# Tying late readers behind the newest weight split in a hybrid mLSTM / DeltaNet block

## The chip, the cores and the metric

One Trainium2 core runs the whole kernel as one program. The time is device time in microseconds (us) of one execution, from a few repeated runs; a separate profiled execution gives the trace. The engines are TensorE (PE, with its weight loads shown as PEld), VectorE (DVE), ScalarE (ACT), GpSimd (POOL) and SyncE (SP), which here does nothing but issue DMA transfers. Each engine works through its own queue of instructions in a fixed order: an instruction that waits holds up all behind it on its engine.

## What is computed

A decoder block on x of 512 tokens by 2048 channels, all in float32. One input projection of the normalized x feeds an mLSTM branch (8 heads), a gated DeltaNet branch (16 heads) and two gates; one output projection brings each branch back to 2048 channels.

```python
u = _rmsnorm(h, norm_w)
proj = jnp.matmul(u, w_in)                 # 2048 x 20528
# mLSTM: q, k, v, o, z, i, f       DeltaNet: q, k, v, z, b, a       gates: a, b
...
h_a = _rmsnorm(_mlstm_chunkwise(...)) * ml_norm_w * sigmoid(ml_o) * silu(ml_z)
...
dq, dk, dv = split(_causal_conv_silu(dn_qkv, dn_conv_w), 3)
h_b = _rmsnorm(_gated_delta_chunkwise(l2(dq), l2(dk), dv, beta, g), dn_norm_w) * silu(dn_z)
...
y = sigmoid(gate_a) * (h_a @ w_out[:2048]) + sigmoid(gate_b) * (h_b @ w_out[2048:])
out = _rmsnorm(x + y, final_norm_w)
```

The delta rule solves, for each chunk, a unit lower triangular system; `_causal_conv_silu` is a depthwise convolution over 4 tokens followed by SiLU.

## The kernel before

**Products with split weights.** Each float32 matrix product is made of three products of rounded parts: a tile `raw` is loaded (`load_raw`, L146), ACT writes its rounded copy `hi` (`split_hi`, L113, tile wh), DVE the remainder `lo` (`split_lo`, L116, tile wl). `next_w` (L158) hands out the parts of block i and, before that, traces the loads up to block i+4 and the splits up to block i+3. There are four buffers of each, so split i+3 needs PE to be through block i-1. Splits and loads carry a high priority.

**Order of the work.** UNITS lists four mLSTM units (two heads each) and eight DeltaNet units (two heads each), as mLSTM, DeltaNet, DeltaNet, four times. A DeltaNet unit (`dn_unit`, L698) projects K, Q, V and Z one after the other with `proj_cm` (L201): each is 16 ticks long, and a tick follows each six products (L212 to L214). All other work of the heads is written as Python generators. `start(gen, wait)` puts one on a list; `tick()` resumes those that are due, and what a generator yields is the number of ticks until its next step. So the small work is traced in between the projections' products.

PE's order is the order of this text (`manual_schedule` for PE). The orders of ACT, DVE, POOL and of SP's transfers are made by a planner at build time: it simulates the engines' times and, whenever an engine is free, takes the ready instruction with the highest priority, which is the place in the text, moved forward by `urgent()` and `high_priority`. An instruction may therefore be issued long before its place in the text, if the simulation finds it ready and the engine free. On the chip the order is fixed, and semaphores do the waiting.

**A DeltaNet unit.** `conv_silu` (L436) copies a projection from PSUM (L440, tile yp, on ACT), convolves on DVE (L441, L443), takes tanh on ACT (L446) and finishes SiLU on DVE (L447). `turn` (L464) transposes blocks on DVE and lets `travel` (L471) carry them through DRAM (td) to the other layout. `dn_front_k` (L488), started 4 ticks after K, loads a row to all partitions (gb), masks it on POOL (L493) and takes exponentials on ACT (L495, L499) for the decay tile dm; multiplies K by itself (L510, tile pk); scales (L512, L526, tile aq); sends the 32x32 diagonal blocks through DRAM (ld, L529; ls, L539); solves the triangular systems on DVE in 31 steps of two operations (L549, L551, tiles tmp and xi), two steps per tick; sends the result through DRAM again (xd, L559; tt, L560), and 10 ticks later transposes it (L563, tile tn). `dn_front_q` makes K by Q (L571, L574). `dn_back` (L580), started 4 ticks after Z, takes Q's norms on ACT (L462, tile njk), joins the 32x32 inverses to 128x128 ones by four groups of small products (L604, L615, L616, L626, L633), the results of each going through ACT (L609 and so on, tiles s), scales V (L638), and starts `dn_chain` for each head (L656 to L679: products pr, pw, pst, po). `gated` (L482) multiplies a head's output by its gate and stores it; it is started 12 ticks after the output's `turn`.

**An mLSTM unit.** `ml_prep` (L731) loads two rows, masks, takes exponentials (em, L740) and multiplies K by Q (L745); `ml_rec` (L757) runs the recurrence over four chunks (pnum, pcs, c) and normalizes; `ml_fin` turns the result and starts `gated`.

**At the start**, x is loaded, its sums of squares are taken, each row block is scaled (L281 to L285: DVE, POOL, then DVE and ACT for one half each), and PE transposes it (L291). The first raw tiles are loaded in the same time.

PSUM has three banks for projections (pj), three for small products (wk) and two more (o).

Of the kernel before, what the change touches and what calls it, by code (L numbers as in the profile page):

```python
# [15 lines left out]
P = 128  # L16
S = 512
NC = S // P
# [30 lines left out]
def hybrid_body(  # L49
# [59 lines left out]
        V.tensor_scalar(out=convc, in0=pt[:, 64:256], scalar1=0.5, scalar2=None, op0=ALU.mult)  # L109


    def split_hi(hi, src):
        A.copy(hi, src)  # L113

    def split_lo(lo, src, hi):
        V.tensor_tensor(out=lo, in0=src, in1=hi.bitcast(F32), op=ALU.subtract)  # L116


    plan = []
# [49 lines left out]
    def urgent(level=1):  # L169
        return tc.high_priority(offset=level * PRIO)  # L170
# [4 lines left out]
    def start(gen, wait=0):  # L175
        active.append([gen, clock["t"] + wait])
# [96 lines left out]
    for c in range(NC):  # L273
        xt = xts[c]
        jk = p0.tile([P, HD], F32, tag="jk", name="jk", bufs=2)
        A.activation(jk, xt[:, 0:HD], AF.Square, accum_out=ss[:, c, 0:1])
        jv = p0.tile([P, HD], F32, tag="jv", name="jv", bufs=2)
        V.scalar_tensor_tensor(out=jv, in0=xt[:, HD:D], scalar=1.0, in1=xt[:, HD:D], op0=ALU.mult, op1=ALU.mult,
                               accum_out=ss[:, c, 1:2])
        V.tensor_tensor(out=rs[:, c:c + 1], in0=ss[:, c, 0:1], in1=ss[:, c, 1:2], op=ALU.add)  # L280
        V.tensor_scalar(out=rs[:, c:c + 1], in0=rs[:, c:c + 1], scalar1=1.0 / D, scalar2=EPS,  # L281
                        op0=ALU.mult, op1=ALU.add)
        G.tensor_tensor(out=rs[:, c:c + 1], in0=rs[:, c:c + 1], in1=mhalf[:, c:c + 1], op=ALU.pow)
        V.tensor_scalar(out=xt[:, 0:HD], in0=xt[:, 0:HD], scalar1=rs[:, c:c + 1], scalar2=None, op0=ALU.mult)
        A.mul(xt[:, HD:D], xt[:, HD:D], rs[:, c:c + 1])  # L285

    def make_u(kt):
        pool, tg = ((psw, "wk"), (pso, "o"))[kt % 2]
# [139 lines left out]
    def row_bcast(r, name):  # L428
        t = wk.tile([P, NC, P], F32, tag="rb", name=name, bufs=3)
        nc.sync.dma_start(t.rearrange("p c t -> p (c t)"), rows_d[r, :].partition_broadcast(P))  # L430
        return t

    def bc(col, n):
        return col.unsqueeze(2).to_broadcast([P, NC, n])

    def conv_silu(ps, ct, dst):  # L436
        yp = yps[cnt["yp"] % NYP]
        cnt["yp"] += 1
        with urgent():
            A.copy(yp[:, 3:S + 3], ps)  # L440
        V.tensor_scalar(out=dst, in0=yp[:, 3:S + 3], scalar1=convc[:, 144 + ct:145 + ct], scalar2=None, op0=ALU.mult)  # L441
        for j in (2, 1, 0):
            V.scalar_tensor_tensor(out=dst, in0=yp[:, j:j + S], scalar=convc[:, 48 * j + ct:48 * j + ct + 1], in1=dst,  # L443
                                   op0=ALU.mult, op1=ALU.add)
# [12 lines left out]
    def token_norms(pk, dst):  # L457

        jk = wk.tile([P, P], F32, tag="jk", name="njk", bufs=1)
        for c in range(NC):  # L460
            with urgent():
                A.activation(jk, pk[:, c, :], AF.Square, accum_out=dst[:, c:c + 1])  # L462
# [17 lines left out]
        yield 1  # L480

    def gated(hn, w, g, kt):  # L482
        V.scalar_tensor_tensor(out=g, in0=hn.rearrange("p c t -> p (c t)"), scalar=w, in1=g, op0=ALU.mult,
                               op1=ALU.mult)
        nc.sync.dma_start(h_d[kt], g)
        yield 1

    def dn_front_k(hs, kq, u):  # L488
        for j in range(2):
            h = hs[j]  # L490
            rb = row_bcast(16 + h, "gb")
            dm = wk.tile([P, NC, P], F32, tag="dm", name="dm")
            G.affine_select(out=dm, in_=rb, pattern=[[0, NC], [1, P]], channel_multiplier=-1, base=0,  # L493
                            compare_op=ALU.is_ge, fill=-1e30)
            A.activation(rb, rb, AF.Exp)  # L495
            ge = wk.tile([P, NC], F32, tag="ge", name="ge", bufs=4)
            V.tensor_copy(ge, rb[:, :, P - 1])
            for c in range(NC):
                A.activation(dm[:, c, :], dm[:, c, :], AF.Exp, bias=ngam[:, c, h:h + 1])  # L499
# [41 lines left out]
        G.memset(xi, 0.0)  # L541
        for q in range(4):
            G.memset(xi.rearrange("p m t -> p (m t)")[q * NSYS:(q + 1) * NSYS, q:(BS // 4) * BS:BS + 4], 1.0)
        yield 4
        for i in range(BS - 1):
            n, m = BS - 1 - i, i // 4 + 1
            tmp = wk.tile([P, 80], F32, tag="tmp", name="tmp")
            tv = tmp[:, 0:n * m].rearrange("p (a b) -> p a b", b=n)
            V.tensor_tensor(out=tv, in0=ls[:, i, i + 1:BS].unsqueeze(1).to_broadcast([P, m, n]),  # L549
                            in1=xi[:, 0:m, i].unsqueeze(2).to_broadcast([P, m, n]), op=ALU.mult)  # L550
            V.tensor_tensor(out=xi[:, 0:m, i + 1:BS], in0=xi[:, 0:m, i + 1:BS], in1=tv, op=ALU.subtract)  # L551
            if i % 2:
                yield 1
# [5 lines left out]
                nc.sync.dma_start(xd[:, :, :, q, :].rearrange("g b m t -> (g b) m t"), xi[q * NSYS:(q + 1) * NSYS])  # L559
            nc.sync.dma_start(tt, xd.rearrange("g b m q t -> (b m q) g t"))  # L560
        yield 10
        with urgent():
            V.transpose(tn.rearrange("p g m -> p (g m)"), tt.rearrange("p g t -> p (g t)"))  # L563
        u.update(tn=tn, tt=tt)

# [14 lines left out]
    def dn_back(hs, kq, u):  # L580

        qe = wk.tile([P, 2, NC], F32, tag="qe", name="qe")
        for j in range(2):
            token_norms(u["qn"][j], qe[:, j, :])
        V.tensor_scalar(out=qe, in0=qe, scalar1=EPS, scalar2=EPS * P, op0=ALU.add, op1=ALU.mult)
        u["qe"] = qe
        for j in range(2):
# [47 lines left out]
            V.tensor_copy(tb[0:64, :, 64:128], p4[0:64])  # L635
        for j in range(2):
            vn = u["vs"][j]
            V.tensor_tensor(out=vn, in0=vn, in1=bc(u["nk"][:, j, :], P), op=ALU.mult)  # L638
        start(dn_chain(0, hs, kq, u), 2)
        start(dn_chain(1, hs, kq, u), 3)  # L640

# [56 lines left out]
    def dn_unit(p):  # L698
        hs = (2 * p, 2 * p + 1)
        dcol = p * NB  # L700
        u = {"aq": [], "qt": [], "ke": [], "vs": [], "g": [], "dm": []}
        kq = [wk.tile([P, 2, S], F32, tag="kq", name=f"kq{h}", bufs=4) for h in hs]
        ps = proj_cm(DN_K + dcol)
        for j in range(2):
            conv_silu(ps[j], 16 + hs[j], kq[j][:, 0, :])
            ke = wk.tile([P, NC, P], F32, tag="ke", name="ke", bufs=4)
            turn(kq[j][:, 0, :], ke)
            u["ke"].append(ke)
        start(dn_front_k(hs, kq, u), KWAIT)
        ps = proj_cm(DN_Q + dcol)  # L710
        u["qn"] = []
        for j in range(2):
            conv_silu(ps[j], hs[j], kq[j][:, 1, :])
            qn = wp.tile([P, NC, P], F32, tag="tg", name="qn", bufs=3)
            turn(kq[j][:, 1, :], qn)
            u["qn"].append(qn)
        start(dn_front_q(hs, kq, u), QWAIT)
        ps = proj_cm(DN_V + dcol)
        for j in range(2):
            vt = wk.tile([P, NC, P], F32, tag="vn", name="vt", bufs=4)  # L720
            conv_silu(ps[j], 32 + hs[j], vt.rearrange("p c t -> p (c t)"))
            turn(vt, vt)
            u["vs"].append(vt)
# [33 lines left out]
    def ml_rec(j, hs, kq, u):  # L757
# [2 lines left out]
        kT = kq[j][:, 0, :]  # L760
        w, we, de, qi = u["em"][j]
        kw = u["kw"][j]
        V.tensor_tensor(out=kw, in0=kw, in1=bc(we, P), op=ALU.mult)
        sq = wk.tile([P, NC], F32, tag="sq", name="sq")
        c1 = None
        for c in range(NC):
# [242 lines left out]
```

## Time and profile before

| what | us |
|---|---|
| median of 3 runs | 2394.93 (2393.64 to 2398.55) |
| the profiled execution's own time | 2400.5 |
| its span, first to last instruction | 2398.5 |
| mean granted clock of TensorE | 0.987 |
| DVE busy | 1144.5 |
| ACT busy | 800.1 |

A row of the timeline reads: start in us from the span's start, length, engine (a q behind it is the queue that issues transfers), line of the kernel, operation, tile written <- tiles read, shape, count, and in brackets the idle time of the engine just before and what ended it. A row of the waits reads: who waited <- for whom: us in all, times, the longest. A row of a group of instructions reads: line, engine, operation, tiles, shape and count | busy us, mean ns of one | idle us before and its releasers. A row of a stretch reads: from:to, length, then for PE, PEld, DVE, ACT and POOL the busy us (and instructions), then the granted clock of PE, the DMA share and GB/s.

### The profile page before, as it was taken

The numbers are of one execution on the slowest core, as the hardware profiler recorded it, in microseconds if no ns is written. First come the engines' busy times: TensorE is split into PE (matmuls) and PEld (weight loads), VectorE is DVE, ScalarE is ACT, GpSimd is POOL, SyncE is SP. The second block draws the span as 40 slices with busy tenths as digits, with TensorE's granted clock in tenths as the row PEclk, the third lists the DMA queues.
The fourth block names the chain that finished last, engine by engine and source line by source line (L and its number), as shares of the span: only waits on it lengthen the run. The fifth ranks groups of instructions, "written<-read, shape, count | busy, mean of one in ns | idle before, by whom it ended". The sixth has DMA issues, their size and how long they took to land.

```text
span 2398.5 us, 32163 instructions
## 1 busy us (share of the span) xinstructions
PE 2311.6 (96%) x11647; PEld 1927.6 (80%) x11647; DVE 1144.5 (48%) x2347; ACT 800.1 (33%) x1702; POOL 192.6 (8%) x261
## 2 busy tenths in 40 slices
PE   6999989999998999999899999989999999999998
PEld 5888768788877888887787888778998888888886
DVE  4532857433385744248573425847333222434334
ACT  4323333332333433234242323423333322322222
POOL 0000102100010200002020001011000000010010
PEclk9999989999999999999999999999999999999999
DMA  5533645443364645336563534646375543633433
GB/s 145 129 97 101 152 121 143 125 128 97 101 147 123 159 112 132 97 99 154 128 162 96 141 97 108 149 120 156 99 247 148 158 114 116 213 116 119 128 115 130
DMA packets 465441, 313.12 MB, mean 131 GB/s; under 512 B 234113, under 2 KB 404322, under 8 KB 465282
## 3 DMA queue, kind: packets, MB, share of 16 engines
q1 hardware_dynamic: 465218, 311.01, 48.3%
q8 instruction: 91, 1.49, 0.3%
q14 instruction: 68, 0.56, 0.1%
q10 hardware_dynamic: 64, 0.07, 0.0%
HBM read 264.77 MB, written 46.20 MB: 130 GB/s over the span
## 4 chain that ended last, share of the span: by engine, by line
PE 80%; DMA 6%; DVE 6%; SPq 4%; issue 2%; ACT 1%; POOL 0%; DVEq 0%; POOLq 0%; ACTq 0%
PE pj L212 13%; PE pj L213 12%; PE pj L214 12%; PE py L944 5%; PE py L943 5%; PE py L942 5%; PE pg L242 4%; PE pg L243 4%; PE pg L244 4%; PE pv L243 2%; PE pv L244 2%; PE pv L242 2%; SPq L476 2%; PE pjt L227 1%; PE pjt L229 1%
## 5 line engine op out<-in xcount | busy, mean ns | idle before, releaser
L116 DVE TENSOR_TENSOR wl<-wr,wh 128x512 fp32r<-128x512 f32 x768 | 538.3, 703 | 849.8 <-ACT wh L113 835.5
L113 ACT CAST wh<-wr 128x512 fp32r<-128x512 f32 x768 | 475.8, 621 | 1237.8 <-PE pj L213 588.1
L212 PE MATMUL pj<-uh,wh 128*128 128x512 f32 x1792 | 735.2, 410 | 10.3 <-ACT yp L440 7.0
L214 PE MATMUL pj<-uh,wl 128*128 128x512 f32 x1792 | 706.3, 394 | 0.0
L213 PE MATMUL pj<-ul,wh 128*128 128x512 f32 x1792 | 706.1, 394 | 0.0
L212 PEld LDWEIGHTS pj<-uh,wh 128*128 128x128 f32 x1792 | 341.6, 191 | 81.4 <-ACT yp L440 10.7
L214 PEld LDWEIGHTS pj<-uh,wl 128*128 128x128 f32 x1792 | 340.6, 190 | 74.3
L213 PEld LDWEIGHTS pj<-ul,wh 128*128 128x128 f32 x1792 | 341.4, 191 | 64.1
L942 PE MATMUL py<-wh,hh 128*128 128x512 f32 x512 | 199.2, 389 | 0.0
L943 PE MATMUL py<-wl,hh 128*128 128x512 f32 x512 | 199.2, 389 | 0.0
L944 PE MATMUL py<-wh,hl 128*128 128x512 f32 x512 | 199.2, 389 | 0.0
L242 PE MATMUL pg<-wh,uh 128*128 128x512 f32 x384 | 149.4, 389 | 0.0
L243 PE MATMUL pg<-wl,uh 128*128 128x512 f32 x384 | 149.4, 389 | 0.0
L244 PE MATMUL pg<-wh,ul 128*128 128x512 f32 x384 | 149.4, 389 | 0.0
L943 PEld LDWEIGHTS py<-wl,hh 128*128 128x128 f32 x512 | 96.1, 188 | 20.1
L942 PEld LDWEIGHTS py<-wh,hh 128*128 128x128 f32 x512 | 96.1, 188 | 20.0
L944 PEld LDWEIGHTS py<-wh,hl 128*128 128x128 f32 x512 | 96.1, 188 | 19.8
L242 PE MATMUL pv<-wh,uh 128*128 128x512 f32 x256 | 99.6, 389 | 0.0
L243 PE MATMUL pv<-wl,uh 128*128 128x512 f32 x256 | 99.6, 389 | 0.0
L244 PE MATMUL pv<-wh,ul 128*128 128x512 f32 x256 | 99.6, 389 | 0.0
L244 PEld LDWEIGHTS pg<-wh,ul 128*128 128x128 f32 x384 | 72.1, 188 | 15.1
L242 PEld LDWEIGHTS pg<-wh,uh 128*128 128x128 f32 x384 | 72.1, 188 | 14.9
(243 smaller groups left out, 2328.2 us busy)
## 6 DMA issues: line engine op xcount, KB each, us to landing
wr<-in_w_in_dram SPq DMA_DIRECT2D x640, 256.0 KB, 2.8
wr<-in_w_out_dram SPq DMA_DIRECT2D x128, 256.0 KB, 3.0
td<-to SPq DMA_DIRECT2D x128, 64.0 KB, 2.0
hr<-h_d SPq DMA_DIRECT2D x32, 256.0 KB, 3.5
tgl<-tg_d SPq DMA_DIRECT2D x32, 256.0 KB, 3.1
tg_d<-tgw SPq DMA_DIRECT2D x24, 256.0 KB, 3.3
xt<-in_x_dram SPq DMA_DIRECT2D x8, 512.0 KB, 7.9
gb<-rows_d SPq DMA_DIRECT2D x16, 256.0 KB, 3.9
```

What stands on the lines that cost most here:

```text
L113: A.copy(hi, src)
L116: V.tensor_tensor(out=lo, in0=src, in1=hi.bitcast(F32), op=ALU.subtract)
L212: T.matmul(ps[j], hi[:, k, wsl], uh[:, kt, :], start=(kt == 0), stop=False)
L213: T.matmul(ps[j], hi[:, k, wsl], ul[:, kt, :], start=False, stop=False)
L214: T.matmul(ps[j], lo[:, k, wsl], uh[:, kt, :], start=False, stop=(kt == KT - 1))
L242: T.matmul(ps[c], uh[:, kt, tsl], hi[:, 0, :], start=(kt == 0), stop=False)
L243: T.matmul(ps[c], uh[:, kt, tsl], lo[:, 0, :], start=False, stop=False)
L244: T.matmul(ps[c], ul[:, kt, tsl], hi[:, 0, :], start=False, stop=(kt == KT - 1))
L476: nc.sync.dma_start(d[:, :, a, :].rearrange("m r c -> r m c"), ov[a * BS:(a + 1) * BS])
L942: T.matmul(ps[c], hh[base][:, kt, tsl], hi[:, 0, :], start=(kt == 0), stop=False)
L943: T.matmul(ps[c], hh[base][:, kt, tsl], lo[:, 0, :], start=False, stop=False)
L944: T.matmul(ps[c], hl[base][:, kt, tsl], hi[:, 0, :], start=False, stop=(kt == KT - 1))
```

## The change

`newest` keeps, for ACT and for DVE, the last split traced so far (at the start: the last scaling of x). `behind(engine)` puts what its block traces behind that instruction in the engine's order, at build time; it adds no instruction and no semaphore. The tie applies to the place in the text: at a tick within block i, the newest split is that of block i+3.

```diff
+    newest = {}
+
     def split_hi(hi, src):
-        A.copy(hi, src)
+        newest["A"] = A.copy(hi, src).ins
 
     def split_lo(lo, src, hi):
-        V.tensor_tensor(out=lo, in0=src, in1=hi.bitcast(F32), op=ALU.subtract)
+        newest["V"] = V.tensor_tensor(out=lo, in0=src, in1=hi.bitcast(F32), op=ALU.subtract).ins
+
+    def behind(eng):
+
+        return tc.issue_after(newest[eng])
...
-            split_hi(hi, raw)
-            split_lo(lo, raw, hi)
+            with ExitStack() as first:
+                if not parts:
+                    first.enter_context(behind("V"))
+                    first.enter_context(behind("A"))
+                split_hi(hi, raw)
+                split_lo(lo, raw, hi)
...
+    def silu_end(dst, then=None):
         th = wk.tile([P, S], F32, tag="th", name="th", bufs=3)
-        A.activation(th, dst, AF.Tanh)
+        with behind("A"):
+            A.activation(th, dst, AF.Tanh)
         V.scalar_tensor_tensor(out=dst, in0=th, scalar=1.0, in1=dst, op0=ALU.add, op1=ALU.mult)
+        if then is not None:
+            turn(*then)
+        yield 1
...
     def dn_front_k(hs, kq, u):
-        for j in range(2):
-            h = hs[j]
-            rb = row_bcast(16 + h, "gb")
+        rbs = [row_bcast(16 + h, "gb") for h in hs]
+        yield 4
+        for j in range(2):
             dm = wk.tile([P, NC, P], F32, tag="dm", name="dm")
-            G.affine_select(out=dm, in_=rb, ...)
-            A.activation(rb, rb, AF.Exp)
+            G.affine_select(out=dm, in_=rbs[j], ...)
+            u["dm"].append(dm)
+        yield 2
+        for j in range(2):
+            h, rb, dm = hs[j], rbs[j], u["dm"][j]
             ge = wk.tile([P, NC], F32, tag="ge", name="ge", bufs=4)
-            V.tensor_copy(ge, rb[:, :, P - 1])
-            for c in range(NC):
-                A.activation(dm[:, c, :], dm[:, c, :], AF.Exp, bias=ngam[:, c, h:h + 1])
-            u["dm"].append((dm, rb, ge))
+            with behind("A"):
+                for c in range(NC):
+                    A.activation(dm[:, c, :], dm[:, c, :], AF.Exp, bias=ngam[:, c, h:h + 1])
+                A.activation(rb, rb, AF.Exp)
+            G.tensor_copy(ge, rb[:, :, P - 1])
+            u["dm"][j] = (dm, rb, ge)
...
-        yield 4
+        yield 7
         for i in range(BS - 1):
...
-            V.tensor_tensor(out=tv, in0=ls..., in1=xi..., op=ALU.mult)
+            with behind("V"):
+                V.tensor_tensor(out=tv, in0=ls..., in1=xi..., op=ALU.mult)
...
         yield 10
-        with urgent():
+        with urgent(), behind("V"):
             V.transpose(tn..., tt...)
...
     def dn_unit(p):
...
         for j in range(2):
+            ke = wk.tile([P, NC, P], F32, tag="ke", name="ke", bufs=4)
+            u["ke"].append(ke)
             conv_silu(ps[j], 16 + hs[j], kq[j][:, 0, :])
-            ke = wk.tile([P, NC, P], F32, tag="ke", name="ke", bufs=4)
-            turn(kq[j][:, 0, :], ke)
-            u["ke"].append(ke)
-        start(dn_front_k(hs, kq, u), KWAIT)
+            start(silu_end(kq[j][:, 0, :], (kq[j][:, 0, :], ke)), 3 + 2 * j)
+        start(dn_front_k(hs, kq, u), 1)
...
     def ml_prep(j, hs, kq, u):
...
         iwb = row_bcast(8 + h, "iwb")
+        yield 4
         em = wk.tile([P, NC, P], F32, tag="dm", name="em")
         G.affine_select(out=em, in_=rb, ...)
-        for c in range(NC):
-            A.activation(em[:, c, :], em[:, c, :], AF.Exp, bias=acol[:, c, h:h + 1])
-        yield 4
+        yield 2
+        with behind("A"):
+            for c in range(NC):
+                A.activation(em[:, c, :], em[:, c, :], AF.Exp, bias=acol[:, c, h:h + 1])
+        yield 2
```

Q and V of a DeltaNet unit end in the same way as K: the convolution stays at its place, and `silu_end` with the `turn` follows 3 and 5 ticks later for the two heads. These operations are tied as well, unmoved in the text: `gated`'s multiplication (L483), the scaling of V in `dn_back` (L638) and of K in `ml_rec` (L763), all behind DVE's newest split, and the norms in `dn_back` (L462) behind ACT's. The last scalings of x (L284, L285) are set as `newest` at the start, so that the first weight split is tied behind them.

More of the change, by code (lines that the diff above doesn't have):

```diff
@@ L283, in hybrid_body @@
         G.tensor_tensor(out=rs[:, c:c + 1], in0=rs[:, c:c + 1], in1=mhalf[:, c:c + 1], op=ALU.pow)
-        V.tensor_scalar(out=xt[:, 0:HD], in0=xt[:, 0:HD], scalar1=rs[:, c:c + 1], scalar2=None, op0=ALU.mult)
-        A.mul(xt[:, HD:D], xt[:, HD:D], rs[:, c:c + 1])
+        newest["V"] = V.tensor_scalar(out=xt[:, 0:HD], in0=xt[:, 0:HD], scalar1=rs[:, c:c + 1], scalar2=None,
+                                    op0=ALU.mult).ins
+        newest["A"] = A.mul(xt[:, HD:D], xt[:, HD:D], rs[:, c:c + 1]).ins
     def make_u(kt):
@@ L482, in gated @@
     def gated(hn, w, g, kt):
-        V.scalar_tensor_tensor(out=g, in0=hn.rearrange("p c t -> p (c t)"), scalar=w, in1=g, op0=ALU.mult,
-                               op1=ALU.mult)
+        with behind("V"):
+            V.scalar_tensor_tensor(out=g, in0=hn.rearrange("p c t -> p (c t)"), scalar=w, in1=g, op0=ALU.mult,
+                                   op1=ALU.mult)
         nc.sync.dma_start(h_d[kt], g)
@@ L488, in dn_front_k @@
     def dn_front_k(hs, kq, u):
+        rbs = [row_bcast(16 + h, "gb") for h in hs]
+        yield 4
         for j in range(2):
-            h = hs[j]
-            rb = row_bcast(16 + h, "gb")
             dm = wk.tile([P, NC, P], F32, tag="dm", name="dm")
-            G.affine_select(out=dm, in_=rb, pattern=[[0, NC], [1, P]], channel_multiplier=-1, base=0,
+            G.affine_select(out=dm, in_=rbs[j], pattern=[[0, NC], [1, P]], channel_multiplier=-1, base=0,
                             compare_op=ALU.is_ge, fill=-1e30)
-            A.activation(rb, rb, AF.Exp)
+            u["dm"].append(dm)
+        yield 2
+        for j in range(2):
+            h, rb, dm = hs[j], rbs[j], u["dm"][j]
             ge = wk.tile([P, NC], F32, tag="ge", name="ge", bufs=4)
-            V.tensor_copy(ge, rb[:, :, P - 1])
-            for c in range(NC):
-                A.activation(dm[:, c, :], dm[:, c, :], AF.Exp, bias=ngam[:, c, h:h + 1])
-            u["dm"].append((dm, rb, ge))
+            with behind("A"):
[4 more added lines that the diff above has]
+            u["dm"][j] = (dm, rb, ge)
         nk = wk.tile([P, 2, NC], F32, tag="nk", name="nk")
@@ L548, in dn_front_k @@
             tv = tmp[:, 0:n * m].rearrange("p (a b) -> p a b", b=n)
-            V.tensor_tensor(out=tv, in0=ls[:, i, i + 1:BS].unsqueeze(1).to_broadcast([P, m, n]),
-                            in1=xi[:, 0:m, i].unsqueeze(2).to_broadcast([P, m, n]), op=ALU.mult)
+            with behind("V"):
+                V.tensor_tensor(out=tv, in0=ls[:, i, i + 1:BS].unsqueeze(1).to_broadcast([P, m, n]),
+                                in1=xi[:, 0:m, i].unsqueeze(2).to_broadcast([P, m, n]), op=ALU.mult)
             V.tensor_tensor(out=xi[:, 0:m, i + 1:BS], in0=xi[:, 0:m, i + 1:BS], in1=tv, op=ALU.subtract)
@@ L582, in dn_back @@
         qe = wk.tile([P, 2, NC], F32, tag="qe", name="qe")
-        for j in range(2):
-            token_norms(u["qn"][j], qe[:, j, :])
+        with behind("A"):
+            for j in range(2):
+                token_norms(u["qn"][j], qe[:, j, :])
         V.tensor_scalar(out=qe, in0=qe, scalar1=EPS, scalar2=EPS * P, op0=ALU.add, op1=ALU.mult)
@@ L637, in dn_back @@
             vn = u["vs"][j]
-            V.tensor_tensor(out=vn, in0=vn, in1=bc(u["nk"][:, j, :], P), op=ALU.mult)
+            with behind("V"):
+                V.tensor_tensor(out=vn, in0=vn, in1=bc(u["nk"][:, j, :], P), op=ALU.mult)
         start(dn_chain(0, hs, kq, u), 2)
@@ L714, in dn_unit @@
             qn = wp.tile([P, NC, P], F32, tag="tg", name="qn", bufs=3)
-            turn(kq[j][:, 1, :], qn)
             u["qn"].append(qn)
+            start(silu_end(kq[j][:, 1, :], (kq[j][:, 1, :], qn)), 3 + 2 * j)
         start(dn_front_q(hs, kq, u), QWAIT)
@@ L720, in dn_unit @@
             vt = wk.tile([P, NC, P], F32, tag="vn", name="vt", bufs=4)
+            u["vs"].append(vt)
             conv_silu(ps[j], 32 + hs[j], vt.rearrange("p c t -> p (c t)"))
-            turn(vt, vt)
-            u["vs"].append(vt)
+            start(silu_end(vt.rearrange("p c t -> p (c t)"), (vt, vt)), 3 + 2 * j)
         ps = proj_cm(DN_Z + dcol)
@@ L738, in ml_prep @@
                         compare_op=ALU.is_ge, fill=-1e30)
-        for c in range(NC):
-            A.activation(em[:, c, :], em[:, c, :], AF.Exp, bias=acol[:, c, h:h + 1])
-        yield 4
+        yield 2
+        with behind("A"):
+            for c in range(NC):
+                A.activation(em[:, c, :], em[:, c, :], AF.Exp, bias=acol[:, c, h:h + 1])
+        yield 2
         psc = psw.tile([P, NC, P], F32, tag="wk", name="psc")
@@ L762, in ml_rec @@
         kw = u["kw"][j]
-        V.tensor_tensor(out=kw, in0=kw, in1=bc(we, P), op=ALU.mult)
+        with behind("V"):
+            V.tensor_tensor(out=kw, in0=kw, in1=bc(we, P), op=ALU.mult)
         sq = wk.tile([P, NC], F32, tag="sq", name="sq")
```

## The prediction

> **What bounds the kernel now.** I read the page first, for who is busy, and then the waits of the tensor engine, for where it is not.
>
> ```profile
> span 2398.5 us, 32163 instructions
> ...
> PE 2311.6 (96%) x11647; PEld 1927.6 (80%) x11647; DVE 1144.5 (48%) x2347; ACT 800.1 (33%) x1702; POOL 192.6 (8%) x261
> ```
>
> PE is busy for 2311.6 of 2398.5 us, so only what makes PE wait, or run slowly, can be won. None of the waits below is for a weight split: the splits run three blocks ahead.
>
> ```profile
> PE p L604 <- DVE tn L563: 33.7, 7, 8.1
> ...
> PE pnum L770 <- DVE c L780: 7.8, 4, 3.0
> PE pj L212 <- ACT yp L440: 7.0, 7, 2.5
> PE put L291 <- DVE xt L284: 5.6, 1, 5.6
> PE pj L212 <- ACT thz L454: 3.1, 2, 1.7
> ```
>
> The largest is L604, the first product of dn_back: it waits for tn, the end of the triangular solve, in 7 of 8 DeltaNet units. The timeline of PE shows the worst one (first DeltaNet unit, behind an mLSTM unit):
>
> ```profile
> 327.36 0.39 PE L214 MATMUL pj<-uh,wl 128*128 128x512 f32 x1
> 335.88 1.06 PE L604 MATMUL p<-tn,aq 32*32 32x32 f32 x32 [8.13 <-DVE tn L563]
> ...
> 337.46 0.63 PE L213 MATMUL pj<-ul,wh 128*128 128x512 f32 x1
> 337.89 0.63 PE L214 MATMUL pj<-uh,wl 128*128 128x512 f32 x1
> ...
> 341.26 0.39 PE L213 MATMUL pj<-ul,wh 128*128 128x512 f32 x1
> 341.49 0.40 PE L214 MATMUL pj<-uh,wl 128*128 128x512 f32 x1
> ```
>
> The columns are start and length. Matmuls overlap, so the pace is start to start: 341.49-341.26 = 0.23 us at speed, 337.89-337.46 = 0.43 just after the stall. Some 9 products between 337.46 and 341.26 run at the slow pace, 9 x 0.20 = 1.8 us on top of the 8.1. A tick (six products) is 6 x 0.23 = 1.4 us.
>
> Why tn is late stands in the timelines of DVE and of SP for this unit, whose K projection ended at 240.37 (first yp copy on ACT):
>
> ```profile
> 240.37 0.59 ACT L440 COPY yp<-pj 128x512 f32<-128x512 f32 x1 [1.86 <-PE pj L214]
> ```
> ```profile
> 274.24 0.19 DVE L549 TENSOR_TENSOR tmp<-ls,xi 128x31 f32<-128x31 f32 x1 [3.58 <-DMA ls<-ld]
> ...
> 294.90 0.75 DVE L483 SCALAR_TENSOR_TENSOR mg<-mhn,normc,mg 128x512 f32<-128x512 f32 x1 [2.28 <-DMA mhn<-td]
> ...
> 319.60 0.17 DVE L551 TENSOR_TENSOR xi<-xi,tmp 128x8 f32<-128x8 f32 x1
> ...
> 335.28 0.45 DVE L563 STREAM_TRANSPOSE tn<-tt 128x256 f32<-128x256 f32 x1 [2.85 <-DMA tt<-xd]
> ```
> ```profile
> 326.47 2.94 SPq L559 DMA_DIRECT2D xd<-xi  x4
> ```
> ```profile
> 274.00:320.00 46.00, 43.89 (x193) 35.60 (x192) 41.47 (x114) 21.04 (x58) 4.83 (x5) 0.96 0.60 146
> ```
> ```profile
> L551 DVE TENSOR_TENSOR xi<-xi,tmp 128x60 f32<-128x60 f32 (+24 forms) x31 | 8.3, 266 | 0.6
> L549 DVE TENSOR_TENSOR tmp<-ls,xi 128x60 f32<-128x60 f32 (+24 forms) x31 | 7.5, 242 | 4.1 <-DMA ls<-ld 3.6
> ...
> L443 DVE SCALAR_TENSOR_TENSOR kq<-yp,convc,kq 128x512 f32<-128x512 f32 x4 | 2.9, 745 | 0.0
> ...
> L497 DVE COPY ge<-gb 128x4 f32<-128x4 f32 x2 | 0.3, 164 | 0.0
> ```
>
> The solve starts at 274.24, when ls has landed, and ends at 319.60+0.17 = 319.77: 45.5 us for 8.3+7.5 = 15.8 us of its own work. The row of the stretch 274 to 320 has its third figure for DVE: 41.47 of 46 us busy. So solve steps stand in one queue with everything else, and a reader whose transfer hasn't landed stops them all (2.28 us before mg). Then xd's issue comes 326.47-319.77 = 6.7 us after its data, behind other issues on SP, and the two transfers take 335.28-326.47 = 8.8 us. PE wanted the result at 327.36+0.23 = 327.6.
>
> In the second unit of the pair the same chain is 2.8 us late, with a blocked reader of 4.13 us in its solve:
>
> ```profile
> 416.16 0.75 DVE L483 SCALAR_TENSOR_TENSOR gz<-os,normc,gz 128x512 f32<-128x512 f32 x1 [4.13 <-DMA os<-td]
> ```
> ```profile
> 445.47 0.69 PE L604 MATMUL p<-tn,aq 32*32 32x32 f32 x32 [2.80 <-DVE tn L563]
> ...
> 447.64 0.63 PE L214 MATMUL pj<-uh,wl 128*128 128x512 f32 x1
> 448.07 0.63 PE L212 MATMUL pj<-uh,wh 128*128 128x512 f32 x1
> ```
>
> Over the run, these readers hold up their engines like this (total us, times, longest):
>
> ```profile
> ACT gb L495 <- POOL dm L493: 46.7, 12, 7.0
> ...
> DVE tmp L549 <- DMA ls<-ld: 29.6, 8, 5.6
> ...
> DVE vt L638 <- DMA vt<-td: 28.3, 13, 4.9
> DVE mg L483 <- DMA mhn<-td: 26.2, 11, 3.8
> ```
>
> **The change part by part.** A tie adds no instruction and no semaphore: it only forbids that a reader stands ahead of the newest split at its place in the text. Split i+3 can run as soon as PE is through block i-1, so a tie costs a reader a tick or two, and nothing that has slack notices.
>
> *Readers on DVE (gated, L638, kw, the solve's first operation, tn).* gated, traced 12 ticks (some 16 us) after its transpose, can no longer come early: the 2.28 us in the first unit and 4.13 us in the second leave the solve. I take 3 us per unit, between 0 (the reader was filling a hole) and 4.1. L638 moves behind dn_back's first products; its 28.3 us fall mostly after the solve, so I count them as nothing for tn. The tie of the solve step does not bind: step 0 now has its place at about tick 16 after K (1+4+2 to the products, 1+1 between and behind them, 7 more), some 16 x 1.4 = 22 us plus small products, while ls lands 274.1-240.4 = 34 us after K. So the 29.6 us of L549's wait stay.
>
> *The mLSTM steps.* ml_prep yields 8 instead of 4 for each of two heads, so the second head's normalization, transposes and transfers come 8 ticks, 11 us, later. In the first unit they stood on SP in front of xd: I take 4.5 of the 6.7 us back in the four units behind an mLSTM unit (ends: 0, 6.7), and count the first head's share of DVE, which now moves into the solve, as 2 us against it.
>
> *The front of K.* Before, the decay tile's exponentials ran long before K's end. Now row loads, the mask on POOL, exponentials and products are four steps, and the products come at tick 7 instead of 4: 3 x 1.4 = 4.2 us later. The exponentials stand behind a split on ACT at that tick:
>
> ```profile
> L499 ACT ACTIVATE dm<-dm,ngam 128x128 f32<-128x128 f32 x64 | 20.2, 386 | 0.0
> ...
> L495 ACT ACTIVATE gb<-gb 128x512 f32<-128x512 f32 x16 | 10.1, 633 | 46.7 <-POOL dm L493 46.7
> ```
>
> Busy time is 20.2/8 + 10.1/8 = 3.8 us per unit; of it the second head's products have to await 3.8-0.6 = 3.2 us, mostly beside the three ticks. What waits behind them on ACT is a split with three blocks of cover. So the solve's start moves by about +4 us (0 to 4.2+3.2 = 7.4); as DVE is full there anyway, I let half, 2 us, reach the end (ends: 0, 7.4). ACT gets back up to 46.7 us of blocked time, off the path.
>
> *tanh by itself.* It leaves ACT's queue until 3 and 5 ticks later, 4 and 7 us; by then the four operations of up to 0.745 us that it follows are done, and the products at tick 7 still find kq. ge (16 copies of 0.164 us) goes to POOL: nothing, it is read a chain later.
>
> *Sum for tn.* First units of a pair: -3 -4.5 +2 +2 = -3.5 us of stall each; second ones: -3 +2 = -1. Over four of each that is -18 of the 33.7. A stall that goes takes its slow products along: 1.8 us in perhaps 4 of 8 units, -7.
>
> [...]
>
> *The other stalls.* pnum (7.8 us) waits for c behind the same blocked DVE: 4 us back with its slow products 6, ends 0 and 15. The projection's banks (7.0+3.1 us) wait for ACT: 4 back, ends 0 and 10.
>
> *The start.* The first split now follows the scaling of x:
>
> ```profile
> 17.02 0.15 DVE L280 TENSOR_TENSOR rs<-ss 128x1 f32<-128x1 f32 x1
> 18.64 1.34 ACT L113 CAST wh<-wr 128x512 fp32r<-128x512 f32 x2 [2.77 <-DMA wr<-in_w_in_dram]
> ...
> 19.89 0.15 DVE L281 TENSOR_SCALAR rs<-rs 128x1 f32<-128x1 f32 x1
> ...
> 21.95 0.47 PE L291 MATMUL put<-ident,xt 128*128 128x128 f32 x1 [5.62 <-DVE xt L284]
> ```
>
> L281 could follow L280 at 17.2 but waits behind wl until 19.89: up to 2.7 us. Only the first split is tied, and a second may still stand there: 2 us (0.7 to 2.7).
>
> *What it adds.* dn_back's eight norms leave their early place and stand in front of s1 on ACT:
>
> ```profile
> L462 ACT ACTIVATE njk<-qn 128x128 f32<-128x128 f32 x64 | 19.8, 309 | 17.7 <-DMA qn<-td 16.1
> ...
> L462 ACT ACTIVATION_READ_ACCUMULATOR njk<-qn 128x1 f32 x64 | 12.0, 187 | 0.0
> ```
>
> (19.8+12.0)/8 = 4.0 us per unit, against two ticks (2.8 us) until the next products want s1, with a block's lead before: 0.5 us x 8 = 4 (0 to 10). K's products hold two of the three wk banks until their exponentials are done, while a chain of the unit before wants banks: 0.5 us x 8 = 4 (0 to 24).
>
> Total: -18 -7 -6 -4 -2 +4 +4 = -29. The profiled execution took 2400.5 us (span 2398.5), 5.6 above the median 2394.93, so 2400.5-29 = 2371.5 there and 2394.93-29 = 2366 as a median. That is my forecast; by the ends of the terms it lies between 2335 and 2390.
>
> **The rivals.**
>
> *The solve comes later instead* (slower). If DVE gives the solve no time back, the three ticks and the exponentials reach tn whole: +7.4 us in 8 units = 59, less 8 for start and pnum: 2394.93+51 = 2446; with half of it, 2394.93+29.5-8 = 2416. For it: the solve now has a later place than Q's convolution, which it preceded, and DVE is 41.47 of 46 us busy. Against: both blocked readers and SP's queue stood inside this chain. It decides from the point where the solve's last step comes later than some 79 us after K's end (319.77-240.37).
>
> *The banks* (slower): if exponentials, not products, free the wk banks, PE stands 3 us in each of 8 units: 24, and a sum of -29+20 no longer shows; with the norms at their end too (+6), 2394.93-29+20+6 = 2392, up to 2405 if pnum gains nothing.
>
> *The ties don't bind*: the planner placed the readers at those places already, and waits stay: only the start's 2 us and some reordering, 2385 to 2398. Against: in the trace, readers stand well ahead of their text, as gz at 416.16 does.
>
> *Everything goes*: all 33.7+8 us at tn, 15 at pnum, 10 at the banks, 2.7: 2394.93-69 = 2326.
>
> **How the numbers follow.** Forecast 0.50 (2366, 2335 to 2390), solve later 0.20 (2416 to 2446), banks 0.10 (2392 to 2405), no binding 0.12 (2385 to 2398), everything goes 0.08 (2326). The measurement tells about 0.2%, 4.8 us. Faster: 0.50+0.08, and about half of no binding, 0.06: 0.64. The same: the other half, and a third of banks: 0.09. Slower: 0.20+0.07 = 0.27. The range leaves out the far half of "solve later" (0.10) and "everything goes" (0.08): 2332 to 2432.
>
> **What would show it.** Right: L604's wait for tn under 18 us in all, waits of L483, L638 for transfers nearly gone, xd issued within 3 us of the last solve step, ls's wait still there. Wrong: last solve step later than 79 us after K's first yp copy; new PE waits at L510, L656 or L664 for aq (banks) or at L615 for s. The forecast fails most likely in how much DVE time reaches the solve.

## The result, and the profile after

| | before | after |
|---|---|---|
| median, us | 2395.93 (2393.64 to 2399.1, 8 runs) | 2387.74 (2382.77 to 2391.7, 8 runs) |
| profiled execution, its span | 2400.5, 2398.5 | 2387.62, 2385.8 |
| granted clock | 0.987 | 0.988 |

The ratio is 0.9964, with a 95% interval of 0.9952 to 0.9976: faster by 0.36%, 8.2 us. The forecast was 2366, so the sign was right and the gain came to less than a third of the 29 us.

The waits of the tensor engine after, in the columns of before:

```profile
PE p L629 <- DVE tn L587: 33.5, 8, 7.8
...
PE pj L222 <- ACT yp L451: 7.9, 5, 2.8
PE pj L222 <- ACT thz L471: 4.8, 3, 2.1
PE put L302 <- DVE xt L294: 2.4, 1, 2.4
PE pqk L595 <- DVE kq L461: 0.6, 1, 0.6
```

L629 is the former L604. Its wait for tn was 33.7 and is 33.5. The wait of pnum for c, 7.8 before, is gone, and with it a second row of 1.7 us for the same product, which the prediction did not count. The projections' banks went from 7.0+3.1 = 10.1 to 12.7. The start went from 5.6 to 2.4. Together -0.2 -7.8 +2.6 -3.2 = -8.6, about the 8.2 of the medians. So what is left to explain is why the wait for tn did not shrink.

The first unit again: ACT's first copy of K, then DVE's first and last solve step and tn.

```profile
237.45 0.57 ACT L451 COPY yp<-pj 128x512 f32<-128x512 f32 x1
```
```profile
272.14 0.19 DVE L573 TENSOR_TENSOR tmp<-ls,xi 128x31 f32<-128x31 f32 x1 [3.10 <-DMA ls<-ld]
...
317.98 0.17 DVE L575 TENSOR_TENSOR xi<-xi,tmp 128x8 f32<-128x8 f32 x1
...
331.30 0.45 DVE L587 STREAM_TRANSPOSE tn<-tt 128x256 f32<-128x256 f32 x1 [5.61 <-DMA tt<-xd]
```

The waits of DVE within that solve, 272.2 to 318.2, and the row of the stretch:

```profile
DVE tmp L573 <- DMA ls<-ld: 3.1, 1, 3.1
DVE wl L118 <- ACT wh L115: 2.7, 1, 2.7
```
```profile
272.00:318.00 46.00, 45.50 (x208) 37.26 (x207) 42.05 (x117) 15.85 (x34) 6.52 (x6) 1.00 0.69 167
```

The blocked reader in the solve (mg, 2.28 us before) is gone; what is left are ls and a weight split that waits for ACT. Yet the solve lasts 318.15-272.14 = 46.0 us, against 45.5 before: DVE is busy for 42.05 of 46 us, with 117 instructions where it had 114. In this unit the place that the reader left was filled by other work.

Then SP, in the kernel before and after. Each time these are the eight transfers of the second mLSTM head (td<-mhn), which stand ahead of xd:

```profile
316.71 2.96 SPq L476 DMA_DIRECT2D td<-mhn  x3
...
320.33 2.86 SPq L476 DMA_DIRECT2D td<-mhn  x5
```
```profile
316.42 1.40 SPq L493 DMA_DIRECT2D td<-mhn  x3
317.86 0.71 SPq L152 DMA_DIRECT2D wr<-in_w_in_dram  x1
318.62 1.66 SPq L493 DMA_DIRECT2D td<-mhn  x3
320.39 0.43 SPq L152 DMA_DIRECT2D wr<-in_w_in_dram  x1
320.86 1.13 SPq L493 DMA_DIRECT2D td<-mhn  x2
...
322.63 0.68 SPq L583 DMA_DIRECT2D xd<-xi  x1
...
324.81 2.13 SPq L583 DMA_DIRECT2D xd<-xi  x3
```

xd is issued 322.63-318.15 = 4.5 us after its data. The change had moved the second head 8 ticks, 11 us, later in the text, and yet its transfers still stand in front of xd. Counted from K's first copy, PE's last product for that head comes 12.3 us later (58.6 before, 70.9 after), but DVE's transposes behind it only 5.2 us later (73.1 and 78.2) and the first transfer 2.7 us later (76.3 and 79.0). Before, 14.5 us passed on DVE between that product and the transposes; after, 7.3. As means over the four units behind an mLSTM unit the transposes come 3.6 us later and the first transfer 1.2.

The steps of this chain in all eight units, from the timelines, as means in us after the first copy of K (first units: behind an mLSTM unit; second units: the others; PE is ready 0.23 us after the start of the last product ahead of it):

| | first solve step | end of solve | first xd | tn | PE ready for it | stall |
|---|---|---|---|---|---|---|
| before, first | 34.1 | 80.3 | 85.9 | 94.7 | 87.8 | 7.1 |
| after, first | 34.7 | 79.7 | 84.3 | 93.1 | 85.8 | 7.3 |
| before, second | 29.4 | 75.3 | 77.6 | 86.4 | 85.0 | 1.6 |
| after, second | 35.8 | 78.9 | 79.6 | 86.9 | 85.6 | 1.4 |

The two kinds of units differ. In the second ones the solve starts 6.4 us later and is 2.9 us shorter (43.1 us against 45.9), so its end is 3.6 us later; xd and its way to tn make that up. In the first ones the start moves by 0.6 us only, and tn did come 1.6 us earlier, but PE was ready 2.0 us earlier too. The reason is where the stalls of pnum stood. PE before, in the first of these units:

```profile
298.93 0.70 PE L770 MATMUL pnum<-c,mkq 128*128 128x257 f32 x2 [1.59 <-DVE c L780]
```

Such stalls lie between K's end and the product that waits for tn, in all four first units. PE time saved there is handed to the wait for tn, unless tn itself comes earlier. With their second row the stalls of pnum come to 2.4 us in a first unit; they turned into time only so far as tn came earlier, 1.6 us.

### The profile page after: what moved, and what is told of

It is laid out like the page before. It is cut to its first block, busy times and chain, and to the rows that moved or that the text cites. A ratio compares the mean times of both kernels' runs of the same rounds, so it can differ in the third digit from the quotient of the medians.

```text
span 2385.8 us, 32124 instructions
## 1 busy us (share of the span) xinstructions
PE 2308.0 (97%) x11647; PEld 1926.1 (81%) x11647; DVE 1146.0 (48%) x2331; ACT 802.2 (34%) x1702; POOL 198.2 (8%) x277
## 5 line engine op out<-in xcount | busy, mean ns | idle before, releaser
L118 DVE TENSOR_TENSOR wl<-wr,wh 128x512 fp32r<-128x512 f32 x768 | 547.3, 714 | 910.9 <-ACT wh L115 887.9
L224 PEld LDWEIGHTS pj<-uh,wl 128*128 128x128 f32 x1792 | 340.0, 190 | 74.1
L973 PEld LDWEIGHTS py<-wl,hh 128*128 128x128 f32 x512 | 96.1, 188 | 20.1
L253 PEld LDWEIGHTS pg<-wl,uh 128*128 128x128 f32 x384 | 72.1, 188 | 15.3 <-DVE wl L118 0.5
```

The lines of the kernel that those rows point to most:

```text
L118: newest["V"] = V.tensor_tensor(out=lo, in0=src, in1=hi.bitcast(F32), op=ALU.subtract).ins
L224: T.matmul(ps[j], lo[:, k, wsl], uh[:, kt, :], start=False, stop=(kt == KT - 1))
L253: T.matmul(ps[c], uh[:, kt, tsl], lo[:, 0, :], start=False, stop=False)
L973: T.matmul(ps[c], hh[base][:, kt, tsl], lo[:, 0, :], start=False, stop=False)
```

## The experiments

All kernels compute the same result. Ratios are to the kernel before, on the same chip. That kernel took 2395.93, 2398.94, 2402.35 and 2403.57 us in the four sets of runs, so kernels of different sets are compared by their ratios, and a difference of ratios is turned into us of 2396. After the traces I had two theories for tn. (A) The later front of K takes away what the ties give. (B) The solve steps have lost their place in DVE's order to operations that now come ahead of them. SP, where xd waits, was the third suspect.

**The start alone.** The kernel before with only the first split tied.

```diff
+                if not parts:
+                    first.enter_context(behind("V"))
+                    first.enter_context(behind("A"))
```

> The kernel before with one tie alone: the first weight split behind the last scaling of x. Theory S (the start gives about 3 us of the 8): 2393 us, ratio to before about 0.9988, PE's wait for xt at L291's place 2.4 us instead of 5.6, all else as before. Rival (a second, untied split stands there still and the change after shows a gain from elsewhere): 2395 to 2396, wait 5 us.

Measured: 2397.58, ratio 1.0 [0.9988, 1.0012]. The wait of put fell to 1.9, as theory S had it, and the wait for tn rose from 33.7 to 35.6. Alone it is worth less than 0.12%, 2.9 us.

**The ties alone**, without the new steps: tanh, exponentials and mLSTM steps stay where they were.

> The kernel before with all ties, but with every step at its old place in the text: exponentials, norms, tanh inside conv_silu, ge on DVE, yields of before. Theory A (ties free DVE, the later front of K of the change eats that up): tn comes earlier than before, the wait for tn falls from 33.7 to about 15 to 20 us, pnum's wait goes, time about 2370. Rival B (the solve ends when DVE's queue is worked off, wherever its parts stand): wait for tn 30 to 35 us, time 2385 to 2390. Rival C (ties alone change nothing, the steps do it): 2393, as the first tie alone.

Measured: 2389.67, ratio 0.9966 [0.9954, 0.9978], as much as the whole change. None of the three had PE's wait for tn, which is larger than before:

```profile
PE p L620 <- DVE tn L578: 41.7, 8, 9.1
...
PE pk L524 <- DVE kq L458: 4.7, 4, 1.2
...
PE pnum L789 <- DVE c L799: 3.2, 2, 1.7
```

In the first units the solve lasts 78.1-35.4 = 42.7 us, before 80.3-34.1 = 46.2: the ties shorten it by 3.5, and its end comes 2.2 us earlier; the wait of pnum is down to 3.2. In the second ones nothing (45.7 against 45.9). In the first units xd comes 7.1 us after the solve, where it was 5.6, and PE is ready some 2.5 us earlier; K's products now wait for kq.

**The steps alone**: the kernel after without its ties, except the first split's.

```diff
     def behind(eng):
-        return tc.issue_after(newest[eng])
+        return ExitStack() if parts else tc.issue_after(newest[eng])
```

> The changed kernel without any tie but the first split's: its steps and yields alone. Theory A: the front of K is later and nothing is freed, wait for tn 40 us or more, pnum's wait back at 5 to 10 us, time 2395 to 2410. Rival B: wait for tn 30 to 35 us, pnum's wait back, 2390 to 2396. Rival C: as the changed kernel, 2388.

Measured: 2445.71, ratio 1.0196 [1.0181, 1.0212], 47 us slower than before and slower than any of the three had it. The waits of PE, of DVE over the run, and of DVE in the first solve (272.3 to 325.1):

```profile
PE p L628 <- DVE tn L586: 73.3, 8, 12.9
```
```profile
DVE mg L500 <- DMA mhn<-td: 38.4, 16, 6.4
```
```profile
DVE mg L500 <- DMA mhn<-td: 4.1, 2, 3.2
DVE vt L663 <- DMA vt<-td: 3.4, 2, 1.8
```

The solve starts as late as after (34.9 and 35.8) and ends at 86.6 and 86.2, some 7 us later than after in both kinds of units. So in the changed kernel the ties are worth 7 us of the solve's end per unit. The steps alone move that end by 6.3 us in first units and 10.8 in second ones.

**More room in front of tn.** The kernel after, with dn_back 6 ticks later.

```diff
-        start(dn_back(hs, kq, u), 4)
+        start(dn_back(hs, kq, u), 10)
```

> The changed kernel with dn_back started 10 ticks after Z instead of 4: it takes the wait for tn off PE without moving the solve. Theory A and B alike: six ticks are 8 us or more, the longest wait is 7.8 us, so the wait for tn falls from 33.5 to under 2 us and the slow products behind it go: 33 + about 10, time 2344 to 2352. Rival D (the stall only moves: chains come later, and banks, buffers or the next unit's K wait instead): 2370 to 2390 with new waits at pr, pw or pj.

Measured: 2322.89 (2321.39 to 2326.43), ratio 0.9689 [0.9673, 0.9705], the fastest of all. PE's waits:

```profile
PE pprm L103 <- DMA nrow<-in_ml_norm_w_dram: 15.0, 1, 15.0
PE put L302 <- DVE xt L294: 2.2, 1, 2.2
```

The first is for a load ahead of PE's first work, which every kernel has. Neither tn nor the banks nor pnum are among the rest. By the ratios this is 66 us below the kernel after, and it lies below the forecast's 2344 to 2352. Besides the 33.5 us for tn the banks' 12.7 went too, which leaves some 20 us, twice what the forecast had for slow products; the granted clock of 0.999, against 0.988, fits that. At one of the banks' waits ACT and PE of the kernel after show this:

```profile
412.98 0.62 ACT L115 CAST wh<-wr 128x512 fp32r<-128x512 f32 x1 [7.80 <-DMA wr<-in_w_in_dram]
413.50 0.58 ACT L451 COPY yp<-pj 128x512 f32<-128x512 f32 x1
```
```profile
414.14 0.80 PE L222 MATMUL pj<-uh,wh 128*128 128x512 f32 x1 [2.60 <-ACT yp L451]
```

The copy that empties the bank stands on ACT behind a split whose load is late. Over the run ACT waits 57.0 us for such loads before, 100.8 after, and 40.6 with dn_back later. Why the loads are in time there was not tried.

**The front of K as early as before.** The kernel after, with K's products at tick 4 again. All that follows them, the solve's place in the text among it, moves three ticks with them.

```diff
         rbs = [row_bcast(16 + h, "gb") for h in hs]
-        yield 4
+        yield 2
...
             u["dm"].append(dm)
-        yield 2
+        yield 1
```

> The changed kernel with K's products back at tick 4 (yields of 2 and 1 in dn_front_k instead of 4 and 2; the solve's yield of 7 stays). Theory A (the later front ate what the ties freed): aq is ready some 4 to 5 us sooner after K, the solve ends sooner by about as much, wait for tn 33.5 to about 12 us, time 2355 to 2368. Rival B (the solve's end follows from DVE's full queue, not from its start): solve ends at 78 to 80 us after K as before, wait for tn 30 to 35, time 2385 to 2391.

Measured: 2355.63, ratio 0.9804 [0.979, 0.9817]. PE's waits, and the first unit (K's first copy at 236.19):

```profile
PE pk L533 <- DVE kq L461: 12.9, 11, 2.2
...
PE p L629 <- DVE tn L587: 1.6, 3, 0.8
```
```profile
268.14 0.19 DVE L573 TENSOR_TENSOR tmp<-ls,xi 128x31 f32<-128x31 f32 x1 [3.61 <-DMA ls<-ld]
...
311.19 0.17 DVE L575 TENSOR_TENSOR xi<-xi,tmp 128x8 f32<-128x8 f32 x1
```

The solve ends at 311.36-236.19 = 75.2, after at 80.7. As means, 74.1 against 79.7 in the first units and 75.4 against 78.9 in the second: 5.7 and 3.6 us earlier, where the solve starts 3.8 and 5.8 us earlier. So over both kinds the later start reaches the end whole, 4.6 of 4.8 us. In the first units xd is now issued ahead of the second mLSTM head's transfers, 2.1 us after the solve instead of 4.6, and tn comes 9.2 us earlier in all. The price is that K's products come before kq's SiLU is done, 12.9 us of PE, which also makes PE ready for tn 3.1 us later in the first units. Theory A has the time it named; the wait for tn falls from 33.5 to 1.6, by the earlier solve, by SP and by that later PE together.

**The solve steps first.** The kernel after, with the two operations of each solve step under `urgent()`.

> The changed kernel with both operations of each solve step urgent, ahead of the convolutions in the planner's order, still tied. Rival B: the solve shrinks from 44 us to about 25, paced by its ticks, the wait for tn goes, time 2335 to 2350. Theory A (start and transfers set tn): the end moves by 5 us at most, wait for tn 15 to 25, time 2365 to 2378.

Measured: 2391.18, ratio 0.995 [0.9937, 0.9964]; the wait for tn is 35.9, the solve ends at 79.9 in both kinds. The solve lasts 45.1 us in the first units, as after (45.0). Theory B falls, as far as a higher priority would have mended it; the step's first operation stayed tied. The time that A named did not come either.

**xd first on SP.** The kernel after, with the transfers of xd and tt ahead of other issues.

```diff
-        with urgent():
+        with urgent(3):
```

> The changed kernel with xd's and tt's transfers ahead of all others in the planner's order on SP. If SP's queue holds xd back in the units behind an mLSTM unit (4.6 us from the last solve step to the first issue), it falls to about 1 us, the wait for tn from 33.5 to 20, time 2373 to 2378. If xd is issued there because its data comes that late in the planner's eyes, nothing moves: 2386 to 2390.

Measured: 2367.02, ratio 0.9851 [0.9837, 0.9865]. DVE, SP and PE's wait:

```profile
316.98 0.17 DVE L575 TENSOR_TENSOR xi<-xi,tmp 128x8 f32<-128x8 f32 x1
```
```profile
317.47 2.63 SPq L583 DMA_DIRECT2D xd<-xi  x4
320.14 0.60 SPq L493 DMA_DIRECT2D td<-mhn  x1
```
```profile
PE p L629 <- DVE tn L587: 13.9, 8, 3.3
```

xd is issued 0.3 us after its data, ahead of five of the eight td<-mhn. The end of the solve stays where it was in the first units (80.0), tn comes 5.0 us earlier there (88.1), and the wait falls by 20 us in all, more than was expected. By the ratios that is 27 us below the kernel after and 36 below the one before, where the forecast of the change was 29.

**What the change is worth with room.** The kernel before with dn_back 6 ticks later, by the edit shown above.

> The kernel before with dn_back 10 ticks after Z instead of 4, no ties. If the readers cost something beside tn's lateness, it stays behind the changed kernel with the same 10 ticks (2323) by the start's 1 to 3 us and pnum's 10 to 15: 2333 to 2340, with pnum's wait at 7 us or more. If all that the ties give runs through tn, it is level: 2321 to 2326.

Measured: 2357.26, ratio 0.981 [0.9796, 0.9823], behind the changed kernel by more than either had it.

```profile
PE pnum L770 <- DVE c L780: 8.1, 4, 3.0
PE put L291 <- DVE xt L284: 5.6, 1, 5.6
PE pj L212 <- ACT yp L440: 5.1, 7, 1.8
PE pj L214 <- DVE wl L116: 4.6, 4, 1.5
```

So with tn out of the way the change takes 0.9689/0.981 = 0.988 of the time, worked out from both intervals 0.9856 to 0.9898: about 1.2% or 29 us, against 0.36%. The waits of before other than tn's are all there, and the last row is new: PE now waits 4.6 us for weight splits on DVE, where the readers wait 28.2 us for mhn, 31.3 for os and 28.6 for vt. I take it that the wait for tn had hidden this.

**Which part of it.** Four kernels, all with dn_back 10 ticks after Z: the ties alone (edit of the second experiment), the steps alone (of the third), and the kernel after with the ties of one engine left out but for the first split's.

```diff
-        return tc.issue_after(newest[eng])
+        return ExitStack() if parts and eng == "V" else tc.issue_after(newest[eng])
```

> The kernel before with all ties and none of the new steps, and dn_back 10 ticks after Z instead of 4, so that PE no longer waits for tn. Theory 'ties': once tn has slack, the ties alone give what the whole change gave there (2357 to 2323): pnum's wait goes from 8.1+2.2 us to under 3, the banks' waits under 3, time 2323 to 2337. Rival 'steps': the tanh and the exponentials as steps of their own are needed too, time 2340 to 2357.

> The changed kernel without its ties (the start's kept), and dn_back 10 ticks after Z instead of 4. With the ties away the solve ended some 7 us later (86.6 us after K's first copy) and then 15 us pass until p1; by 101.6 against 93.8 wanted PE should wait again for tn, some 4 to 8 us in the first units of a pair, with pnum's wait back at 6: 2365 to 2385 by theory 'ties'. Rival 'steps': the steps alone carry the gain once tn has slack: no wait for tn, 2323 to 2340.

> The changed kernel with dn_back 10 ticks after Z and only ScalarE's ties kept (tanh, exponentials, norms); VectorE's readers are free again. Theory: it is the readers of transfers on VectorE that delay c (pnum) and the solve, so their waits for mhn, vt and kw come back at 15 to 38 us each and the time is 2345 to 2370. Rival: ScalarE's late results are what counts (the banks' copies stand behind them), 2323 to 2335.

> The changed kernel with dn_back 10 ticks after Z and only VectorE's ties kept; tanh, exponentials and norms on ScalarE are free again. Theory: the gain stays, 2323 to 2335, with some ScalarE waits for gb/dm back (up to 40 us) beside PE's work. Rival: 2340 to 2365, PE waiting for its projection banks (pj for yp) by 5 us or more.

| ties | steps | dn_back after 4 ticks | after 10 ticks |
|---|---|---|---|
| none | old | 1 | 0.981 [0.9796, 0.9823] |
| all | old | 0.9966 [0.9954, 0.9978] | 0.9754 [0.974, 0.9769], 2343.45 us |
| start's | new | 1.0196 [1.0181, 1.0212] | 0.9903 [0.9889, 0.9918], 2379.31 us |
| ScalarE's | new | | 0.9859 [0.9842, 0.9875], 2369.89 us |
| VectorE's | new | | 0.9744 [0.9729, 0.9758], 2340.91 us |
| all | new | 0.9964 [0.9952, 0.9976] | 0.9689 [0.9673, 0.9705], 2322.89 us |

The rows of PE's waits, for ScalarE's ties alone and then for VectorE's alone:

```profile
PE p L629 <- DVE tn L587: 13.9, 4, 3.8
PE pj L224 <- DVE wl L118: 9.1, 12, 1.7
PE pnum L800 <- DVE c L810: 6.9, 4, 2.0
```
```profile
PE pnum L800 <- DVE c L810: 9.1, 4, 2.4
PE p L629 <- DVE tn L587: 3.9, 3, 2.3
PE pj L222 <- ACT yp L451: 3.7, 3, 1.6
```

VectorE's ties are worth the difference between all and ScalarE's alone, 0.9859-0.9689, or 41 us; with them the waits for splits are gone. ScalarE's are worth 0.9744-0.9689, 13 us, on top of VectorE's, and only with both, and with the new steps, are the waits of pnum, tn and the banks all gone: I had expected pnum to follow VectorE's alone, and its time, 2340.91, is at the near edge of the rival's range, though the banks' wait of 3.7 is smaller than the rival's. The ties alone fell into the range of their rival too: with the old steps PE still waits 6.2 us for kq at K's products and 5.1 for tn. The steps alone came out in the time of the first theory, with a wait for tn of 12.0 (1.9 to 3.7 us in a first unit, less than expected). So the ties pay alone, 8 us at 4 ticks and 13 at 10. The steps pay only with the ties: alone they cost 47 us at 4 ticks and 22 at 10, and with the ties they change nothing at 4 and gain 16 at 10.

## Why the prediction was right in its sign and wrong in its size

What did not come are the two largest terms: tn, -18, of which -14 lay in the four first units, and the slow products, -7, that go with it.

- **SP in the first units: this step failed, and it weighs most.** "I take 4.5 of the 6.7 us back in the four units behind an mLSTM unit"; it was 1.0 as a mean (from 5.6 to 4.6), 14 us less over four units. The step took it that 8 ticks in the text carry the second head's transfers out of xd's way. They stand ahead of xd before and after: PE's products moved with the text, but DVE's work behind them had been late and caught up, so the first transfer moved by 1.2 us, not 11. With xd first, the wait for tn falls by 20 us and the ratio is 0.9851.
- **The front of K: this step failed in the second units.** "I let half, 2 us, reach the end" of the solve. There the solve starts 6.4 us later than before, within the range of 0 to 7.4, and its end is 3.6 later, since the solve is 2.9 us shorter, as much as the readers were to give. So the start reached the end whole; with K's products back at tick 4 it also did, as a mean over both kinds. The premise, that DVE is full there anyway, did not make it absorb a late start. In the first units the start moved by 0.6 us only.
- **Readers in the solve, 3 us per unit: about right in size.** The solve is 1.2 us shorter in first units and 2.9 in second ones. The ties alone give 3.5 and 0.2; in the changed kernel, against the steps alone, they bring its end forward by 7 us in both. The waits of L483 and L638 for mhn and vt went from 26.2 and 28.3 us to nothing, as said; gz for os stayed (20.1 before, 20.8 after), though in the second unit's solve it fell from 4.13 us to 0.8.
- **tn, -18, and slow products, -7:** the wait measured 33.7 and 33.5, and the granted clock 0.987 and 0.988, so the slow products stayed with the stalls.
- **pnum, -6:** the wait of 7.8 went whole. But it lies ahead of the wait for tn in the same unit, so the two terms must not be added; I did. PE was ready for tn 2.0 us earlier in each first unit, which used up the 1.6 us by which tn came earlier.
- **The start, -2:** the wait fell by 3.2; alone it was not to be told from nothing.
- **The banks, -4:** the wrong way, +2.6.
- **Norms and wk banks, +4 each:** no such wait at L595 but 0.6 us for kq, none at the others. The rival of the banks did not come about.
- **The solve comes later instead:** the steps alone show its mechanism. There tn comes 6.4 and 6.9 us later, and the time is 47 us above before, where the rival had 7.4 us and 51. The ties bought that back. Its point of decision, 79 us, came from one first unit; as a mean the solve ended there at 80.3 before already, so the figure could decide nothing.
- **ls's wait still there:** right, 22.3 us after 29.6.

What stays open: why DVE's work for the second mLSTM head was late before and not after, why the banks' waits grew, and why the weight loads on ACT are late after (100.8 us of waits) and not with dn_back at 10.

## What to carry to other kernels

Stalls in a row on one engine are not a sum: if a late result is timed from a point ahead of an earlier stall, what is saved at the stall is spent waiting for the result (here the 7.8 us of pnum went, and the wait for tn was 33.7 us before and 33.5 after), so cost the last wait first. When a step is moved by so many ticks in the text, don't take it that its transfers move as far: here 11 us in the text were 1.2 us on SP, so look up what stands ahead of what in every queue. Count a later start of a chain on a full engine (here DVE, 42.05 of 46 us busy) in whole until a run shows otherwise: here 4.6 of 4.8 us reached the end. A change that shows 0.4% behind such a wait showed 1.2% once six ticks of room were given to the result, so before judging it, give the latest result room.

## What the hardware showed that was not expected

How long PE stood idle did not tell by itself, in the waits shown here (1.83 to 2.80 us), whether it came back slow. Two waits for a projection's bank in the kernel after; the first is the one at 414.14 shown above, continued, the second is longer:

```profile
414.73 0.63 PE L223 MATMUL pj<-ul,wh 128*128 128x512 f32 x1
415.16 0.63 PE L224 MATMUL pj<-uh,wl 128*128 128x512 f32 x1
...
824.63 0.50 PE L222 MATMUL pj<-uh,wh 128*128 128x512 f32 x1 [2.80 <-ACT yp L451]
824.97 0.39 PE L223 MATMUL pj<-ul,wh 128*128 128x512 f32 x1
825.20 0.40 PE L224 MATMUL pj<-uh,wl 128*128 128x512 f32 x1
```

Behind 2.60 us of idling the products go at 415.16-414.73 = 0.43 us (granted clock 0.50 from 414.2 to 416.2), behind 2.80 us at 825.20-824.97 = 0.23 us (1.00 from 824.7 to 826.7). With the front of K as early as before, the products behind 1.83 us of waiting for a bank go slowly too:

```profile
1607.01 0.50 PE L222 MATMUL pj<-uh,wh 128*128 128x512 f32 x1 [1.83 <-ACT yp L451]
...
1608.32 0.63 PE L223 MATMUL pj<-ul,wh 128*128 128x512 f32 x1
1608.75 0.63 PE L224 MATMUL pj<-uh,wl 128*128 128x512 f32 x1
```

Here the pace is 1608.75-1608.32 = 0.43 us (granted clock 0.50 from 1608.0 to 1610.5). In the kernel before, the stall at 445.47 is 2.80 us long, as the one at 824.63 is, but its products go at 448.07-447.64 = 0.43 us (granted clock 0.50 from 447.2 to 450.0). The two are not alike: at 445.47 only the 32 small products of L604 follow the wait, so that 446.10-442.67 = 3.43 us pass from the beginning of idling to the next full-size product. The runs don't tell what decides.
